# Pairing six tiles of the recurrent branch's gate, and computing two products of nine gate pairs beside the last attention heads

## The chip, the core and the metric

The kernel runs on one core of a Trainium2 chip. The metric is the device time of one execution in microseconds (us). The kernel before takes 2241.29 us, the median of three runs (2237.54 to 2242.33). The execution that the profiler recorded took 2235.38 us; its span, from the first to the last recorded instruction, is 2233.6 us.

Engines: PE (TensorE, matrix products), DVE (VectorE), ACT (ScalarE), POOL (GpSimd), SP (SyncE, which only issues transfers here). Each works through its own list of instructions in a fixed order. DMA transfers are issued from SP, ACT and POOL.

## The reference

One decoder layer on 1024 tokens of width 1024, in float32. A mixer with three branches reads one combined projection of the input; each branch's projection is multiplied by a sigmoid gate, and their sum goes through an output projection, a layer norm, a SwiGLU feed-forward part and a second layer norm. What the change touches, cut from the reference:

```
proj = x @ w_in
lru_x, lru_gate, qb, kb, vb, qc, kc, vc, gates = jnp.split(proj, split_at, axis=-1)
y_a = rglru_branch(lru_x, lru_gate, ...)       # h * gelu(lru_gate), h from an associative scan
y_b = banded_window_attention(...)             # 16 heads, window 128, sinks
y_c = dilated_attention(qc, kc, vc)            # 16 heads, three dilations
branch = jnp.einsum('bsnc,ncd->bsnd', jnp.stack([y_a, y_b, y_c], axis=2), w_branch)
merged = jnp.sum(jax.nn.sigmoid(gates.reshape(bsz, S, 3, D)) * branch, axis=2)
mix = merged @ w_out
```

`lru_gate` is 1024 channels wide, `gates` 3 x 1024.

## The kernel before

**Products in two parts.** Every float32 operand is split into a rounded part `hi` (a CAST on ACT) and the rest `lo` (a subtraction on DVE, in some stages on POOL), and a product is three matmuls: hi x hi, hi x lo, lo x hi. A tile of 128 output channels by 512 tokens with 1024 inputs is 8 x 3 = 24 matmuls of 128x512. A tile of 128 channels over all 1024 tokens is 48.

**Stages, in time.** (1) The recurrent branch's input, convolution, gates and scan. (2) Sliding-window attention. (3) Dilated attention, eight pairs of heads. In 2 and 3 the heads' small matmuls (scores `s`, transposes `pt`, sums `o`) are interleaved with a "fill" of large matmuls `acc`, taken from a stream of weights `W` (class `WeightStream`): `interleave(pipeline(units), fill, ratio)` takes fill worth 1.7 times the heads' estimated matmul time. (4) The gate pairs. (5) The three branch projections with the sum `merged`. (6) The output projection, layer norm, feed-forward part and second layer norm.

**The recurrent branch's gate** (`lg_job`, `lg_evac`, lines 691 to 720) is eight tiles. Tiles 0 and 1 are fill in stage 2; tiles 2 to 7 are the fill of the last pair of dilated heads, 6 x 48 = 288 matmuls. Each half tile is finished on the spot: ACT Square, DVE two operations, ACT Tanh, DVE two operations, store.

**Gate pairs** (class `Pairs`, lines 802 to 965; set up in lines 967 to 1010). Two tiles of `gates` over all tokens would be 96 matmuls. A pair computes them in seven products of 12 matmuls on sums and differences of blocks (Winograd's form of Strassen): a00, s2, s1, s3, a01, s4, a11, that is 84. The weights' sums t1 to t4 are made by POOL (`wsum`, line 864, and line 901), split by ACT and DVE (`wsplit`, lines 874 and 875), all prepared one pair ahead (`prep`, whose steps `run` places at the points `between(i)`). The raw weights of a pair fill the ring `w_raw` (two buffers), so the next pair's weights can be loaded only when the last step of the present pair's preparation has read them. The x operands s1 to s4 are made at the stage's start from x, loaded into `xq` (`load_xq`, `x_sums` lines 770 to 779, `x_split` lines 987 to 992).

A pair can have its products a00 and a01 done ahead (`front_step`, "fronted"): a01 is added onto a00 in the same bank after a copy of a00 was taken, and the pair itself then is five products, 60 matmuls. Before, pairs 0 to 2 of twelve are fronted, at the start of stage 4. Each of a pair's four results goes through a sigmoid on ACT at once (`sig_out`) and to `sg_dram`; stage 5 loads it (`load_sg`, line 1037) and multiplies.

**Order of instructions.** The framework's scheduler sets the order on every engine from the program's order and a simulated timeline, so an instruction can stand far from where the code names it.

**The start of stage 5** (`load_y`, lines 1019 to 1032): the outputs of a branch are loaded from DRAM, eight tiles per half of the tokens, each with its ACT cast and DVE subtraction right behind the load in the code.

## Time and profile before

| | |
|---|---|
| median of three runs | 2241.29 us |
| profiled execution, its span | 2235.38 us, 2233.6 us |
| PE busy | 2173.8 us (97%) |
| DVE, ACT, POOL busy | 1421.0 us (64%), 962.7 us (43%), 539.8 us (24%) |
| chain that ended last, PE's share | 80% |
| stage 4, first matmul of the fronts to the last gate matmul | 943.04 to 1185.3 us |

Busy time counts the union of an engine's instructions. A 128x512 matmul is recorded with about 390 ns, but matmuls overlap, so time per matmul is read from a stretch: its length over its count. "Idle before" is the time that an engine stood still ahead of an instruction, with the instruction that ended the wait.

### The profile page before, as it was taken

What the parts mean: (1) busy time and instruction counts of PE and PEld (TensorE: products, weight loads), DVE (VectorE), ACT (ScalarE), POOL (GpSimd) and SP (SyncE); (2) the same over time, 40 slices, a digit from 0 to 9 for tenths busy, and PEclk for the clock granted to TensorE, in tenths of its full rate; (3) what the DMA queues carried; (4) which work ended last, traced back from release to release, by engine and by line L of the source; (5) the groups of instructions that cost most, each with busy time, mean ns of one, the idle gap of its engine ahead of it and who ended that gap; (6) DMA issues with size and microseconds to landing.
All of it is one profiled execution on the core that took longest, in us unless ns stands there. A gap on an engine that the chain in (4) does not pass through costs nothing.

```text
span 2233.6 us, 29700 instructions
## 1 busy us (share of the span) xinstructions
PE 2173.8 (97%) x11017; PEld 1840.5 (82%) x11017; DVE 1421.0 (64%) x2685; ACT 962.7 (43%) x1825; POOL 539.8 (24%) x493
## 2 busy tenths in 40 slices
PE   8999999999999999989999999999999999999998
PEld 6787888988889888868887888888788888888786
DVE  7888888776777778764444244449665444553735
ACT  4764766665655655543333102223333333342421
POOL 2332222222222133143220000002444433400301
PEclk9999999999999999999999999999999999999999
DMA  5123123112222143343336334244332222254543
GB/s 151 48 81 97 46 67 78 51 48 66 47 58 56 29 107 121 104 147 121 113 123 214 125 113 132 85 147 143 107 104 85 85 85 85 85 193 144 187 160 118
DMA packets 216449, 232.15 MB, mean 104 GB/s; under 512 B 11056, under 2 KB 160624, under 8 KB 216304
## 3 DMA queue, kind: packets, MB, share of 16 engines
q1 hardware_dynamic: 175504, 130.57, 19.2%
q0 software_dynamic: 18336, 57.73, 8.6%
q10 hardware_dynamic: 22464, 41.95, 5.6%
q8 instruction: 87, 1.43, 0.3%
q14 instruction: 58, 0.48, 0.1%
HBM read 170.43 MB, written 49.28 MB: 98 GB/s over the span
## 4 chain that ended last, share of the span: by engine, by line
PE 80%; DVE 8%; issue 4%; DMA 4%; ACT 2%; POOL 1%; SPq 0%; ACTq 0%; DVEq 0%; POOLq 0%
PE acc L186 68%; PE o L186 4%; PE s L186 4%; PE pt L543 4%; DVE xc L386 1%; DVE w_lo L97 1%; POOL t L864 1%; DMA xin<-in_x_t_dram 1%; DMA w_raw<-in_w_branch_dram 1%; DMA yl<-y_dram 1%; DVE r L1217 0%; DVE xc L383 0%; DVE r L1214 0%; DMA w_raw<-in_w_ffn_in_dram 0%; DVE pt_l L548 0%
## 5 line engine op out<-in xcount | busy, mean ns | idle before, releaser
L186 PE MATMUL acc<-xh,w_hi 128*128 128x512 f32 x760 | 303.3, 399 | 12.9 <-ACT w_hi L96 7.8
L186 PE MATMUL acc<-xl,w_hi 128*128 128x512 f32 x760 | 300.5, 395 | 0.0
L186 PE MATMUL acc<-xh,w_lo 128*128 128x512 f32 x760 | 300.0, 395 | 0.0
L96 ACT CAST w_hi<-w_raw 128x1024 fp32r<-128x1024 f32 x127 | 133.5, 1051 | 298.4 <-PE acc L186 256.4
L874 ACT CAST ph<-t 128x512 fp32r<-128x512 f32 x136 | 82.9, 621 | 243.0 <-POOL t L864 149.8
L97 DVE TENSOR_TENSOR w_lo<-w_raw,w_hi 128x1024 fp32r<-128x1024 f32 x89 | 114.4, 1285 | 102.9 <-ACT w_hi L96 102.6
L186 PEld LDWEIGHTS acc<-xh,w_hi 128*128 128x128 f32 x760 | 143.9, 189 | 40.9 <-ACT w_hi L96 7.8
L864 POOL TENSOR_TENSOR t<-w_raw 128x512 f32<-128x512 f32 x68 | 97.0, 1427 | 312.0 <-DMA w_raw<-in_w_ffn_in_dram 194.1
L186 PEld LDWEIGHTS acc<-xh,w_lo 128*128 128x128 f32 x760 | 143.7, 189 | 28.3 <-DVE w_lo L97 0.8
L186 PEld LDWEIGHTS acc<-xl,w_hi 128*128 128x128 f32 x760 | 143.8, 189 | 25.7
L547 ACT CAST pt_h<-pt 128x512 fp32r<-128x512 f32 (+3 forms) x256 | 124.7, 500 | 89.2 <-PE pt L543 84.2
L548 DVE TENSOR_TENSOR pt_l<-pt,pt_h 128x512 fp32r<-128x512 f32 (+3 forms) x256 | 144.3, 572 | 19.5 <-ACT pt_h L547 17.3
L875 DVE TENSOR_TENSOR pl<-t,ph 128x512 fp32r<-128x512 f32 x136 | 102.9, 762 | 82.3 <-ACT ph L874 82.1
L538 POOL DMA_DIRECT2D y_dram<-yp x96 | 52.2, 543 | 418.2 <-DVE yp L537 323.3
L543 PE MATMUL pt<-ident,p 128*128 128x128 f32 x816 | 128.8, 276 | 2.6 <-DVE pt_l L548 1.6
L186 PE MATMUL o<-pt_h,v 128*128 128x256 f32 (+1 forms) x464 | 117.3, 275 | 1.8 <-DVE yp L537 1.8
L630 ACT ACTIVATE p<-p,small 128x128 f32<-128x128 f32 (+7 forms) x128 | 99.5, 778 | 39.8 <-DVE small L627 38.5
L186 PE MATMUL acc<-w_lo,gh 128*128 128x512 f32 x288 | 112.5, 391 | 4.0 <-DVE w_lo L97 3.9
L186 PE MATMUL o<-pt_l,v 128*128 128x256 f32 (+1 forms) x464 | 113.9, 286 | 1.4 <-DVE pt_l L548 1.4
L97 POOL TENSOR_TENSOR w_lo<-w_raw,w_hi 128x1024 fp32r<-128x1024 f32 x38 | 91.4, 2406 | 97.5 <-ACT w_hi L96 91.4
L186 PE MATMUL acc<-w_hi,gl 128*128 128x512 f32 x288 | 112.1, 389 | 0.0
L186 PE MATMUL s<-kh,q 128*128 128x256 f32 (+3 forms) x320 | 103.8, 333 | 1.0 <-DVE small L572 0.5
(378 smaller groups left out, 5825.0 us busy)
## 6 DMA issues: line engine op xcount, KB each, us to landing
w_raw<-in_w_in_dram SPq DMA_DIRECT2D x79, 512.0 KB, 3.9
w_raw<-in_w_ffn_in_dram SPq DMA_DIRECT2D x48, 512.0 KB, 3.8
w_raw<-in_w_ffn_out_dram SPq DMA_DIRECT2D x47, 512.0 KB, 3.7
sg_dram<-e ACTq DMA_DIRECT2D x48, 256.0 KB, 2.7
w_raw<-in_w_branch_dram SPq DMA_DIRECT2D x24, 512.0 KB, 4.7
sg<-sg_dram POOLq DMA_DIRECT2D x24, 512.0 KB, 3.7
g_dram<-e POOLq DMA_DIRECT2D x44, 256.0 KB, 3.2
yl<-y_dram ACTq DMA_DIRECT2D x32, 256.0 KB, 5.7
```

The source lines that it names most:

```text
L96: self.nc.scalar.copy(hi, raw)
L97: self.lo_engine.tensor_sub(lo, raw, hi.bitcast(F32))
L186: pe.matmul(o, a, b, start=start, stop=stop, skip_group_check=True)
L386: dve.scalar_tensor_tensor(xc, xr[:, 1 + j:1 + j + S], vec[:, j * 8 + ct:j * 8 + ct + 1], xc, op0=OP.mult, op1=OP.add)
L538: pool.dma_start(dst, yp[:, :n])
L543: pe.transpose(pt[:, i * P:(i + 1) * P], b, ident)
L547: act.copy(dst_h, v)
L548: dve.tensor_sub(dst_l, v, dst_h.bitcast(F32))
L630: act.activation(p[:, :n], p[:, :n], AF.Exp, bias=m, scale=-1.0, accum_out=sm[:, 1:2])
L864: pool.tensor_tensor(t, a, b, op=op)
L874: act.copy(hi, src)
L875: dve.tensor_sub(lo, src, hi.bitcast(F32))
```

## The change

1. Tiles 2 to 7 of the recurrent branch's gate are no longer fill. They become three pairs (tiles 2 and 3, 4 and 5, 6 and 7) among the gate pairs, at places 3, 6 and 9 of now fifteen, with seven products each. Their four results go through `lg_finish`, a shorter form with three DVE operations and two ACT ones, in tiles `u` and `hh` that lie in `lgt`.
2. The fill of the last dilated heads is now `tail_front` for the gate pairs 3 to 11: products a00 and a01, 24 matmuls each, with the copy of a00 stored to a new DRAM tensor `p1_dram` and the sum to `sg_dram`. All twelve gate pairs are now fronted; the nine get their a00 back by a load one pair ahead.
3. The sigmoid moves out of the gate pairs: raw gates go to `sg_dram`, and stage 5 applies one 128x1024 sigmoid in place after each load (`sigmoids`).
4. `load_y` only issues its loads, not ahead of the latest weight cast of a pair; the casts and subtractions are handed out one at a time (`y_split`). The first is called four pairs before the end, the second half of the first branch inside the first step of stage 5.
5. In `Pairs` the last preparation step is at point 0 instead of 1, the load at 1 instead of 2, the first sums at 3 instead of 4. The difference a01 of the later x tiles goes from POOL to DVE.

```diff
+    def lg_finish(ct, hf, z, u, hh):
+        act.activation(u, z, AF.Square, scale=math.sqrt(0.044715))
+        dve.scalar_tensor_tensor(u, u, 1.0, z, op0=OP.add, op1=OP.mult)
+        act.activation(u, u, AF.Tanh, scale=math.sqrt(2.0 / math.pi))
+        dve.scalar_tensor_tensor(u, u, 1.0, z, op0=OP.add, op1=OP.mult)
+        dve.scalar_tensor_tensor(u, u, 0.5, hh, op0=OP.mult, op1=OP.mult)
+        pool.dma_start(y_dram[0][ct, :, hf * HALF:(hf + 1) * HALF], u)
...
+    def tail_front(g):
+        def f(hi, lo):
+            acc = acc_ps.tile([P, HALF], F32, tag="acc", name="acc")
+            for q, (tag, dst) in enumerate((("kh", p1_dram[g]), ("kl", sg_dram[2 * g, :, :HALF]))):
+                sl = slice(q * HALF, (q + 1) * HALF)
+                yield from quarter(acc, xops[("a00", "a01")[q]], hi[:, sl], lo[:, sl], q == 0)
+                t = att4.tile([P, HALF], F32, tag=tag, name="front")
+                act.copy(t, acc)
+                act.dma_start(dst, t)
+        W.add([gate_cols(g)[0]], [(0, f)])
...
-            for ct in range(KT):
-                if ct not in EARLY:
-                    lg_job(ct)
+            for g in range(NG, NP):
+                tail_front(g)
...
-        pool.tensor_sub(a01, a01, a00)
+        eng.tensor_sub(a01, a01, a00)
...
             def p6():
-                wsplit(j, "b11", b(1, 1))
                 t = raws[j, "t2"]
                 pool.tensor_sub(t, b(1, 0), t)
+                wsplit(j, "b11", b(1, 1))
                 wsplit(j, "t4", t)
...
-                    if i == 1:
+                    if i == 0:
                         cur[6]()
                     elif nxt:
-                        for f in {2: nxt[:1], 4: nxt[1:3], 5: nxt[3:4], 6: nxt[4:6]}.get(i, ()):
+                        for f in {1: nxt[:1], 3: nxt[1:3], 5: nxt[3:4], 6: nxt[4:6]}.get(i, ()):
...
+    kinds = ["g"] * (NP + 3)
+    for i, j in enumerate((3, 6, 9)):
+        kinds[j] = 2 * i + 2
...
+    def pair_out(j, c, hf, src):
+        if j in gid:
+            if hf == 0 and c == 0:
+                t = gate.temp()
+                act.copy(t, src)
+                src = t
+            act.dma_start(sg_dram[2 * gid[j] + c, :, hf * HALF:(hf + 1) * HALF], src)
+        else:
+            u, hh = [t[:, 2 * hf + c, :] for t in lgt]
+            lg_finish(kinds[j] + c, hf, src, u, hh)
...
         for k in range(KT):
-            raw = yl[k].bitcast(F32)
-            act.dma_start(raw, y_dram[n][k, :, hf * HALF:(hf + 1) * HALF])
-            act.copy(yh[k], raw)
-            dve.tensor_sub(yl[k], raw, yh[k].bitcast(F32))
+            d = act.dma_start(yl[k].bitcast(F32), y_dram[n][k, :, hf * HALF:(hf + 1) * HALF])
+            tc.add_manual_dep(d.ins, recent[-1].ins.name, NO_SYNC, reason="not earlier than the pairs' weights")
+            ysplits.append(lambda k=k: split(k))
...
+    def sigmoids():
+        while fresh:
+            t = fresh.pop(0)
+            act.activation(t, t, AF.Sigmoid)
...
+        if i == 3 and j + 1 in gid and gid[j + 1] >= NG:
+            t = gring.tile([P, HALF], F32, tag="p1", bufs=NG, name="p1")
+            act.dma_start(t, p1_dram[gid[j + 1]])
+            gate.front[j + 1] = t
-        if (j, i) == (9, 0):
+        if (j, i) == (len(kinds) - 4, 0):
             load_y(order[0], 0)
+        elif i in (1, 2, 4, 6):
+            y_split()
```

Three places show what the scheduler makes of it.

PE at the end of the dilated heads: `acc` is fill, `s` and `o` are the heads' own. Before, the last fill matmul stands ahead of a 512 wide score of the last head:

```order
L186 MATMUL acc<-xh_94,w_hi 128x512
L186 MATMUL acc<-xl_96,w_hi 128x512
L186 MATMUL acc<-xh_94,w_lo 128x512
L186 MATMUL s<-kh,q 128x512
L186 MATMUL s<-kl,q 128x512
L186 MATMUL o<-pt_h,v 128x256
```

Now, on PE at the same end of the heads, the last fill matmul stands ahead of a 256 wide score:

```order
L187 MATMUL acc<-xh_94,w_hi 128x512
L187 MATMUL acc<-xl_96,w_hi 128x512
L187 MATMUL acc<-xh_94,w_lo 128x512
L187 MATMUL s<-kh,q 128x256
L187 MATMUL s<-kl,q 128x256
L187 MATMUL o<-pt_h,v 128x256
```

The fill ends earlier among the last head's units: in the list before, 41 fill matmuls still follow that 256 wide score, in the new one none.

DVE at the start of stage 4, from the last head's sum `yp` on (`xq` are sums of x, `gs2l` to `gs4l` and `xl` the lo parts of the operands s1 to s4, `pl` of weights). Before:

```order
L778 TENSOR_TENSOR xq<-xq 128x512
L992 TENSOR_TENSOR gs4l<-xq,gs4h 128x512
L776 TENSOR_TENSOR xq<-xq 128x512
L992 TENSOR_TENSOR gs2l<-xq,gs2h 128x512
L992 TENSOR_TENSOR gs3l<-xq,gs3h 128x512
L992 TENSOR_TENSOR gs4l<-xq,gs4h 128x512
L992 TENSOR_TENSOR xl_96<-xq,xh_94 128x512
L777 TENSOR_TENSOR xq<-xq 128x512
L992 TENSOR_TENSOR gs3l<-xq,gs3h 128x512
L992 TENSOR_TENSOR gs2l<-xq,gs2h 128x512
L992 TENSOR_TENSOR gs4l<-xq,gs4h 128x512
L992 TENSOR_TENSOR xl_96<-xq,xh_94 128x512
```

Now, on DVE from the same `xq` on:

```order
L806 TENSOR_TENSOR xq<-xq 128x512
L1029 TENSOR_TENSOR gs4l<-xq,gs4h 128x512
L804 TENSOR_TENSOR xq<-xq 128x512
L1029 TENSOR_TENSOR gs2l<-xq,gs2h 128x512
L1029 TENSOR_TENSOR gs3l<-xq,gs3h 128x512
L1029 TENSOR_TENSOR gs4l<-xq,gs4h 128x512
L807 TENSOR_TENSOR xq<-xq 128x512
L1029 TENSOR_TENSOR xl_97<-xq,xh_95 128x512
L805 TENSOR_TENSOR xq<-xq 128x512
L1029 TENSOR_TENSOR gs3l<-xq,gs3h 128x512
L1029 TENSOR_TENSOR gs2l<-xq,gs2h 128x512
L1029 TENSOR_TENSOR xl_97<-xq,xh_95 128x512
```

Line 807, the difference a01, is new on DVE; the `gs4l` that needs it has moved back, behind the first weights `pl` of a pair.

POOL at the same place, from the last store of the heads on. Before, the two differences of line 779 stand ahead of and among the weights' sums `t`:

```order
L538 DMA y_dram_59<-yp 64x256 x2
L779 TENSOR_TENSOR xq<-xq 128x512
L864 TENSOR_TENSOR t<-w_raw 128x512
L864 TENSOR_TENSOR t<-w_raw,t 128x512
L779 TENSOR_TENSOR xq<-xq 128x512
L901 TENSOR_TENSOR t<-w_raw,t 128x512
```

Now POOL goes from the stores to the weights' sums:

```order
L539 DMA y_dram_59<-yp 64x256 x6
L887 TENSOR_TENSOR t<-w_raw 128x512
L887 TENSOR_TENSOR t<-w_raw,t 128x512
L923 TENSOR_TENSOR t<-w_raw,t 128x512
L887 TENSOR_TENSOR t<-w_raw 128x512 x2
```

The two differences are gone from POOL's list.

## Rows read from the trace of the kernel before

**Rows 1.** Windows: PE, PEld, DVE, ACT, POOL busy (x count), clock, DMA share, GB/s

```profile
915.70:943.04 27.34, 24.05 (x138) 20.71 (x137) 24.03 (x57) 16.76 (x33) 4.14 (x7) 0.94 0.24 78
943.04:985.00 41.96, 32.83 (x134) 25.33 (x134) 29.21 (x41) 22.44 (x41) 17.86 (x9) 0.96 0.50 164
985.00:1185.34 200.34, 200.34 (x876) 165.56 (x877) 88.05 (x122) 72.98 (x117) 55.20 (x42) 0.99 0.38 121
1185.34:1212.00 26.66, 23.27 (x102) 18.65 (x100) 16.48 (x25) 14.65 (x25) 2.17 (x4) 0.98 0.87 302
1212.00:1366.00 154.00, 154.00 (x668) 127.27 (x669) 53.51 (x70) 19.50 (x24) 7.39 (x14) 0.98 0.37 116
```

**Rows 2.** Chain of waits, in order of time: start, length, what (count)

```profile
1049.96 130.12 PE acc L186 x574
```

**Rows 3.** DVE instructions, the last heads: start, length, what

```profile
917.44 0.56 DVE L627 CUSTOM_DVE_ANT_0 p<-s,dil_mask 128x384 f32<-128x384 f32 x1 [0.16 <-PE pt L543]
923.33 0.69 DVE L706 TENSOR_TENSOR gelu__10106<-gelu__10106,z 128x512 f32<-128x512 f32 x1
930.94 1.23 DVE L97 TENSOR_TENSOR w_lo<-w_raw,w_hi 128x1024 fp32r<-128x1024 f32 x1 [0.31 <-ACT w_hi L96]
```

**Rows 4.** PE instructions that waited, start of stage 4

```profile
943.04 0.45 PE L186 MATMUL acc<-xh,w_hi 128*128 128x512 f32 x1
961.79 0.79 PE L186 MATMUL acc<-xh,ph 128*128 128x512 f32 x1 [4.89 <-ACT p L831]
972.00 0.50 PE L186 MATMUL acc<-gs2l,ph 128*128 128x512 f32 x1 [0.73 <-DVE gs2l L992]
985.00 0.50 PE L186 MATMUL acc<-gs2h,ph 128*128 128x512 f32 x1 [3.46 <-ACT ph L874]
```

**Rows 5.** POOL instructions, the last heads and the start of stage 4

```profile
825.39 1.32 POOL L779 TENSOR_TENSOR xq<-xq 128x512 f32<-128x512 f32 x1
953.38 6.40 POOL L779 TENSOR_TENSOR xq<-xq 128x512 f32<-128x512 f32 x1 [8.51 <-DVE xq L778]
981.15 1.80 POOL L864 TENSOR_TENSOR t<-w_raw 128x512 f32<-128x512 f32 x1 [10.96 <-DMA w_raw<-in_w_in_dram]
983.04 1.26 POOL L864 TENSOR_TENSOR t<-w_raw,t 128x512 f32<-128x512 f32 x1
```

**Rows 6.** DVE instructions, start of stage 4

```profile
948.94 0.69 DVE L776 TENSOR_TENSOR xq<-xq 128x512 f32<-128x512 f32 x1 [4.88 <-DMA xq<-in_x_t_dram]
957.37 0.68 DVE L992 TENSOR_TENSOR gs3l<-xq,gs3h 128x512 fp32r<-128x512 f32 x1
957.98 0.68 DVE L992 TENSOR_TENSOR gs2l<-xq,gs2h 128x512 fp32r<-128x512 f32 x1
960.46 1.09 DVE L992 TENSOR_TENSOR gs4l<-xq,gs4h 128x512 fp32r<-128x512 f32 x1 [1.80 <-ACT gs4h L991]
```

**Rows 7.** Chain of waits, a pair's weights: stage 4's second pair, then the feed-forward part

```profile
973.81 7.18 DMA w_raw<-in_w_in_dram
984.33 0.63 ACT ph L874
...
1580.84 1.68 POOL t L901
1585.82 3.62 DMA w_raw<-in_w_ffn_in_dram
1593.70 1.68 POOL t L901
```

**Rows 8.** ACT instructions: start of stage 4, then of stage 5

```profile
954.03 1.28 ACT L978 ACT_TABLE_LOAD   x1
961.64 1.14 ACT L1030 CAST yv<-yv 128x512 fp32r<-128x512 f32 x2
...
1208.18 1.04 ACT L96 CAST w_hi<-w_raw 128x1024 fp32r<-128x1024 f32 x1
```

**Rows 9.** What PE waited for at the start of stage 5: total, times, longest

```profile
PE acc L186 <- ACT w_hi L96: 2.0, 1, 2.0
PE acc L186 <- DVE w_lo L97: 1.4, 1, 1.4
```

More of the change, by code (lines that the diff above doesn't have):

```diff
@@ new lines, in quarter @@
+    def quarter(bank, a, bh, bl, start):
+        ah, al = a
+        for k in range(4):
+            wh, wl = bh[:, k * P:(k + 1) * P], bl[:, k * P:(k + 1) * P]
+            mm(bank, wh, ah[:, k, :], start and k == 0, False)
+            mm(bank, wh, al[:, k, :], False, False)
+            mm(bank, wl, ah[:, k, :], False, k == 3)
+            if k % 2:
+                yield 1296
+    def tail_front(g):
[8 more added lines that the diff above has]
+        W.add([gate_cols(g)[0]], [(0, f)])
@@ L812, in product @@
         def product(self, bank, op, bh, bl, start):
[L814 to L821 removed]
+            return quarter(bank, self.ops[op], bh, bl, start)
         def bank(self):
@@ L1061, in branch_evac @@
             load_sg(i + AHEAD)
+        else:
+            sigmoids()
     def branch_step(i, hf):
@@ L1088, in at @@
     def at(j, i):
-        if (j, i) == (9, 0):
+        if i == 0 and j not in gid:
+            for hf in range(2):
+                for c in range(2):
+                    load_h(kinds[j] + c, hf, lgt[1][:, 2 * hf + c, :])
+        if i == 3 and j + 1 in gid and gid[j + 1] >= NG:
[3 more added lines that the diff above has]
+        if (j, i) == (len(kinds) - 4, 0):
             load_y(order[0], 0)
-        if (j, i) == (11, 4):
+        elif i in (1, 2, 4, 6):
+            y_split()
+        if (j, i) == (len(kinds) - 1, 3):
             W.prefetch(W.n_dma + 2)
-    gate.run(12, at, first, 2)
+    gate.run(len(kinds), at, first, 2)
     gS.close()
@@ L1101, in trunk_kernel @@
         load_sg(i)
-    load_y(order[0], 1)
     for n_, end in enumerate(ends):
-        for _ in W.run(end):
-            pass
+        for i, _ in enumerate(W.run(end)):
+            if (n_, i) == (0, 0):
+                while ysplits:
+                    y_split()
+                load_y(order[0], 1)
+                sigmoids()
+            y_split()
         if n_ % 7 == 1 and n_ < 14:
```

88 lines of the change are left out of this document (41 added, 47 removed).

## The prediction

> **What bounds the kernel now.** I read the page's busy shares first: PE is busy for 97% of the span, and the chain that ended last is 80% PE. So the time is PE's work plus the few places where PE stands still, and an edit on another engine counts only where PE waits for it. The windows by stage then show where that is [rows 1]. From 985.00 to 1185.34, the gate pairs, PE is busy without a gap; from 943.04 to 985.00, the start of stage 4, it is busy for 32.83 of 41.96 us; at the start of stage 5 for 23.27 of 26.66 us. The price of one large matmul comes from the chain: 574 in 130.12 us, 0.2267 us each [rows 2] (the recorded 390 ns overlap). Over the gate pairs it is 200.34 / 876 = 0.2287 us [rows 1]; I use 0.227. Last I read the waits at the start of stage 4, engine by engine [rows 4 to 6].
>
> **The change, part by part.**
>
> *Fill of the last heads.* It goes from 6 x 48 = 288 matmuls to 9 x 24 = 216. The 72 that go are worth 72 x 0.227 = 16.3 us, as long as PE has other work at the heads' end. The order shows that 41 matmuls (9.3 us) are taken from behind the last 256 wide score, where the heads then stand alone. Before, that stretch lasts from 915.70 to 943.04, 27.34 us. Without the 41 it is 27.34 - 9.3 = 18.0 us if the waits in it stay as they are. Two sums bound it from below: PE's own work there is 24.05 - 9.3 = 14.8 us, and DVE's is 24.03 less what is not the heads' (by the kinds of [rows 3]: twelve operations of the recurrent gate, 3 x (0.42 + 0.69 + 0.68 + 0.68) = 7.4; two splits of x, 1.4; a weight's lo part, 1.2), so 14.0 us. Both are below 18.0, so DVE's relief may pay for the missing cover. Against that, scores, transposes and sums of the last units follow each other through three engines; at worst the waits grow by 4 us. I take a loss of 1, with 0 and 4 as ends. The nine copies of a00 on ACT, between a front's two products in one bank, lie beside the heads' matmuls; they are inside these ends.
>
> *Start of stage 4.* Let E be the end of the heads' matmuls, 943.04 before. From there to the second pair's first matmul at 985.00 PE has 72 matmuls of fronts and 60 of the first pair, 132 x 0.227 = 29.9 us, in 41.96 us: 12 us lost, of which 4.89 + 0.73 + 3.46 are the waits of [rows 4] and the rest is the lower clock (0.96 mean) and the ramp. The longest wait, 4.89 us, is for an ACT copy that stands behind a `gs4h` cast, which waits for POOL's difference a01: that took 6.40 us against 1.32 elsewhere [rows 5]. During it DVE ran subtractions on SBUF operands one behind the other, 0.61 us from start to start [rows 6].
> The change puts this difference on DVE, and takes the early casts of y (961.64 in [rows 8]) away from between the weights' casts. What is late next: DVE starts at E + 5.9 as before, when the x tiles land [rows 6]; the order has 17 instructions ahead of the first weight split `pl`, so 17 x 0.61 = 10.4, to E + 16.3. POOL's two sums for it (t1, t2) fall into this train of DVE. If POOL gets no turn beside it, as in the 6.40 us row, they run after it: 1.80 + 1.26 [rows 5], then ACT 0.63 [rows 7] and DVE 0.69, to E + 20.7. PE has finished its fronts at E + 16.3, so it waits 4.4 us, and ends the first pair at E + 34.3. The second pair's weights can be loaded when the first pair's last splits are done, eight DVE instructions later (E + 25.5); the landing took 7.18 us here and 3.62 elsewhere [rows 7], then POOL 3.1, ACT and DVE 1.3: E + 34 to E + 37. I take E + 35 for the second pair's start, against E + 42 before: 7 us gained. Bounds: 11 if POOL runs beside DVE and the load is short; 3 if every transfer takes 7.2 us and a further wait of 2 to 3 us remains.
> Here a rule of the Trainium skill bears ("SBUF — State Buffer", section "Who interferes with whom"): a DVE instruction with two SBUF inputs and a GpSimd instruction that reads SBUF share a port pair, held by one of them for a whole instruction while the other blocks. The 6.40 us row agrees with it. It speaks against taking the whole 11 us: by it POOL's sums pay what the difference paid; without it the gain here would be 11 and the total 19.
>
> *Gate pairs.* Before, from the second pair on: two of five products and nine of seven, 120 + 756 = 876 matmuls. Now eleven of five and three of seven, 660 + 252 = 912. 36 more x 0.227 = 8.2 us of loss. Beside the fill's gain this is the net saving of the algorithm, 36 matmuls. The new pairs' ends (two ACT and three DVE operations per result, four results, about 0.65 us each) come to 8 us of DVE in a pair of 84 x 0.227 = 19.1 us; DVE is busy for 88.05 of 200.34 us here [rows 1], so they lie beside PE. The sigmoids that leave relieve ACT by 48 x 0.6 us, which bounds nothing. What has little room is a pair's weights: in the feed-forward part, where this loop is itself the chain, one turn from `t` to `t` takes 1593.70 - 1580.84 = 12.86 us with a load of 3.62 us in it [rows 7], against 60 x 0.227 = 13.6 us of PE. The new load of a00 and the loads of `hh` come on top of the traffic. I take 1 us of loss; ends 0 and 7.
>
> *Start of stage 5.* PE waits 3.4 us there for the third and fourth weights [rows 9]: their casts stand behind casts of y that wait for loads (1208.18 in [rows 8]; the first branch product ran at 1185.3). Now the x tiles of the first half are free after the last recurrent pair, so eight of those 24 loads and casts come ahead of stage 5. Added in front of the third weight on ACT: a table load, 1.28 us [rows 8], and one or two sigmoids of about 1.1 us, which wait for their own loads. I take a gain of 2; ends: 3.4 gained, 2 lost. Later in stage 5 ACT is busy for 19.50 of 154 us [rows 1], and the 24 sigmoids lie beside PE.
>
> *The rest* (one DVE operation less per half of the two early tiles, the points in `Pairs` for the feed-forward part) falls where PE is busy all the time; 0, within 1 either way.
>
> Sum: -16.3 + 1 - 7 + 8.2 + 1 - 2 = -15.1 us. The profiled execution took 2235.38 us (span 2233.6), so 2220.3 for one like it. The median of the runs is 2241.29, 5.9 above that execution; with it, 2226.
>
> **The rivals.**
>
> *The entry is freed wholly.* POOL runs beside DVE, the heads' end keeps its length, stage 5 starts without a wait: -16.3 - 11 + 8.2 - 3.4 = -22.5, 2219. For it: POOL's other sums next to busy DVE took 1.3 to 1.8 us. Against it: the 6.40 us.
>
> *The covers fail.* The last heads alone lose 4, the entry gives 3, stage 5's start loses 2 behind the sigmoids: -16.3 + 4 - 3 + 8.2 + 1 + 2 = -4.1, 2237, no change that can be told. For it: in the naked end of the heads each unit needs three engines in turn; the first sigmoid waits for a transfer at a time when the transfers moved 302 GB/s [rows 1]. Against it: DVE has 10 us less to do there.
>
> *The weights' loop becomes the bound* (the other side). Eight pairs that follow a five-product pair are new to this loop (places 5, 6, 8, 9 and 11 to 14). If their loads take the 7.18 us of [rows 7] instead of 3.62, a turn is 16.4 us, 2.8 above PE's 13.6: 8 x 2.8 = 22.4 lost, +7.3 in all, 2249. It decides from a turn of 13.6 + 15.1 / 8 = 15.5 us on. For it: the new transfers, and POOL's stores of `u` that stand ahead of the sums and wait for DVE. Against it: the pairs that run so before show no gap in PE [rows 1], and 7.18 was measured beside the y loads that move away.
>
> **Chances.** The forecast 0.55 (its own range 2220 to 2232), the freed entry 0.17, failing covers 0.18, the weights' loop 0.10, a part of it with small losses. A measurement of this kernel can tell about 0.2%, 4.5 us, from no change. Faster by more: 0.55 + 0.17 + about half of the failing covers, 0.81; within: 0.12; slower: 0.07. The range for 8 in 10 reaches from the freed entry with some run-to-run spread, 2214, into the loop's case, 2243.
>
> **What would show it.** In the changed profile: 36 large matmuls fewer in all; the stretch from the last 256 wide score to the heads' end near 18 us; from there to the second pair's first matmul near 35 us, with POOL's first `t` long or late beside DVE; PE without gaps in the gate pairs and the turns of `t` at 13.6 us; at the start of stage 5 under 1.5 us of waiting. The forecast is wrong if PE waits for `ph` or `pl` in every five-product pair, or if the heads' end takes over 22 us.

## The result and the profile after

The changed kernel takes 2242.52 us (median of 20 runs, 2237.01 to 2248.11) against 2236.32 us for the kernel before in the same series: ratio 1.0022, 95% interval [1.0012, 1.0031]. It is slower by about 5 us. The forecast was 15.1 us less than before, 2226 from a median of 2241.29 that rested on three runs. The profiled execution took 2241.2 us with a span of 2239.4 us, 5.8 above the span before, so the two profiles can stand for the two medians.

The windows by stage of the changed kernel, in the columns of [rows 1]: the last heads alone, the start of stage 4 up to the second pair, the pairs from there on, the start of stage 5, its later part.

```profile
912.00:929.36 17.36, 12.39 (x80) 9.66 (x81) 13.97 (x39) 9.47 (x21) 2.09 (x4) 1.00 0.18 54
929.36:965.81 36.45, 32.74 (x135) 25.58 (x134) 23.00 (x35) 16.06 (x30) 13.84 (x8) 0.95 0.51 161
965.81:1193.08 227.27, 214.63 (x913) 174.87 (x912) 130.00 (x192) 67.18 (x113) 80.01 (x66) 0.97 0.49 155
1193.08:1219.74 26.66, 25.54 (x112) 20.50 (x111) 16.16 (x26) 15.54 (x24) 2.16 (x4) 1.00 0.84 294
1219.74:1368.74 149.00, 149.00 (x659) 123.39 (x658) 51.90 (x68) 35.08 (x38) 7.41 (x14) 1.00 0.38 117
```

The second and third line answer the question. The heads end 13.68 us earlier (929.36 against 943.04), and the second pair starts 36.45 us after that, not 41.96. Then the pairs, which ran without a gap before, take 227.27 us instead of 200.34, with 12.6 us in which PE stands still and a clock of 0.97. (PE's list puts 15 branch matmuls ahead of the last gate product; 1193.08 is the end of the gate pairs less these 15 x 0.2267 us.)

| stretch, profiled executions | forecast | measured |
|---|---|---|
| up to the heads' end | -16.3 + 1 = -15.3 | -13.7 |
| heads' end to the second pair | -7 | -5.5 |
| second pair to the last gate product | +8.2 + 1 = +9.2 | +26.9 |
| stage 5 (to the output projection: 268.98, now 262.98) | -2 | -6.0 |
| the rest (779.28, now 783.34) | 0 | +4.1 |
| sum | -15.1 | +5.8 |

PE's waits in the pairs, in the form of [rows 4]; in brackets the idle time and what ended it. `ph` and `pl` are the hi and lo parts of a pair's weights or of their sums `t`, `b11` is the last block of the raw weights, and `e` stands for the sums that DVE makes of a pair's products.

```profile
949.90 0.50 PE L187 MATMUL acc<-gs2h,ph 128*128 128x512 f32 x1 [3.19 <-ACT ph L897]
978.10 0.50 PE L187 MATMUL acc<-gs2h,ph 128*128 128x512 f32 x1 [1.25 <-ACT ph L897]
1026.87 0.80 PE L187 MATMUL acc<-gs2h,ph 128*128 128x512 f32 x1 [4.71 <-ACT ph L897]
1079.15 0.50 PE L187 MATMUL acc<-gs2h,ph 128*128 128x512 f32 x1 [2.98 <-ACT ph L897]
1130.40 0.50 PE L187 MATMUL acc<-gs2h,ph 128*128 128x512 f32 x1 [3.02 <-ACT ph L897]
1176.58 0.50 PE L187 MATMUL acc<-gs2h,ph 128*128 128x512 f32 x1 [0.67 <-ACT ph L897]
```

Each is the first product (s2) of a pair whose weights are not there. Two of them (949.90 and 978.10) belong to the start of stage 4 and its third pair. The three long ones behind those come two places after each recurrent pair (places 5, 8 and 11). Behind each, the granted clock is down for some time, here behind the first:

```profile
1020.00:1030.00 10.00, 5.29 (x17) 3.97 (x16) 6.70 (x10) 1.77 (x3) 5.31 (x6) 0.79 0.55 194
1030.00:1040.00 10.00, 10.00 (x40) 8.12 (x39) 5.05 (x8) 2.81 (x4) 0.81 (x1) 0.86 0.46 135
1060.00:1070.00 10.00, 10.00 (x46) 8.29 (x45) 7.75 (x12) 4.22 (x8) 3.14 (x3) 1.00 0.28 80
```

In the second line PE is busy throughout and does 40 matmuls, in the third 46: these are means of 10 us, between the levels of 1.2 and 2.4 GHz. From 1026.87 to 1030.00, right behind the wait, the granted clock is 0.50; behind the other two it is 0.71 from 1079.15 to 1085.00 and 0.64 from 1130.40 to 1135.00. So 26.9 us are 36 matmuls (8.2), 12.6 of waits, and the remaining 6.1 are matmuls that took longer than 0.2267 us each, 7.9 us in all against 1.8 before.

What makes ph late is a loop. Here the chain of waits of the changed kernel (start, length, what), a turn near the end of the pairs where nothing disturbs it:

```profile
1155.54 0.61 DVE pl L898
...
1156.21 3.67 DMA w_raw<-in_w_in_dram
...
1160.05 1.30 POOL t L887
...
1161.42 1.30 POOL t L887
...
1164.16 1.68 POOL t L923
1165.84 1.26 POOL t L887
...
1168.39 0.70 DVE pl L898
...
1169.14 3.90 DMA w_raw<-in_w_in_dram
...
1173.21 1.30 POOL t L887
```

The last split of a raw tile (`pl` at 1168.39) frees it, the next pair's weights are loaded into it, POOL makes the sums, and the splits follow: 13.16 us from `t` to `t`. A pair of five products is 13.6 us of PE. The loop is the chain here, though PE waits for it only 0.67 us, at 1176.58. Now POOL's first `t` of the pairs around the first recurrent pair, and then around the second:

```profile
961.67 1.29 POOL L887 TENSOR_TENSOR t<-w_raw 128x512 f32<-128x512 f32 x1 [7.05 <-DMA w_raw<-in_w_in_dram]
974.75 1.29 POOL L887 TENSOR_TENSOR t<-w_raw 128x512 f32<-128x512 f32 x1 [5.75 <-DMA w_raw<-in_w_in_dram]
...
1003.59 1.29 POOL L887 TENSOR_TENSOR t<-w_raw 128x512 f32<-128x512 f32 x1 [8.33 <-DMA w_raw<-in_w_in_dram]
...
1023.57 1.26 POOL L887 TENSOR_TENSOR t<-w_raw 128x512 f32<-128x512 f32 x1 [4.67 <-DMA w_raw<-in_w_in_dram]
...
1040.74 1.29 POOL L887 TENSOR_TENSOR t<-w_raw 128x512 f32<-128x512 f32 x1 [9.94 <-DMA w_raw<-in_w_in_dram]
1055.89 1.29 POOL L887 TENSOR_TENSOR t<-w_raw 128x512 f32<-128x512 f32 x1 [8.11 <-DMA w_raw<-in_w_in_dram]
1075.85 1.26 POOL L887 TENSOR_TENSOR t<-w_raw 128x512 f32<-128x512 f32 x1 [4.63 <-DVE u L697]
1092.58 1.29 POOL L887 TENSOR_TENSOR t<-w_raw 128x512 f32<-128x512 f32 x1 [9.49 <-DMA w_raw<-in_w_in_dram]
```

Undisturbed 13.1 us, across a recurrent pair 20.0 (1003.59 to 1023.57, 1055.89 to 1075.85). One recurrent pair with its two gate pairs is 84 + 60 + 60 matmuls, 46.2 us of PE; the three turns from 1040.74 to 1092.58 take 51.8. The long turn itself, on ACT and then on DVE and SP:

```profile
1010.93 0.62 ACT L897 CAST ph<-t 128x512 fp32r<-128x512 f32 x1 [3.52 <-POOL t L887]
1011.46 0.63 ACT L694 ACTIVATE u<-e 128x512 f32<-128x512 f32 x1
...
1014.90 0.63 ACT L696 ACTIVATE u<-u 128x512 f32<-128x512 f32 x1 [0.87 <-DVE u L695]
1015.44 0.60 ACT L897 CAST ph<-w_raw 128x512 fp32r<-128x512 f32 x1
```

```profile
1016.77 0.69 DVE L898 TENSOR_TENSOR pl<-w_raw,ph 128x512 fp32r<-128x512 f32 x1
```

```profile
1017.52 0.37 SPq L882 DMA_DIRECT2D w_raw<-in_w_in_dram  x1
```

The cast of b11, which has had its data since 1003.6, stands in ACT's list behind Square and Tanh of the recurrent pair's finish; DVE's half of it comes 13.2 us after the first `t` (8.6 us in an undisturbed turn), and the load takes another 6.1 us from its issue to the next `t` (3.7 undisturbed).

### The profile page after: what moved, and what is told of

The parts are those of the page before. It is cut to its first block, busy times and chain, and to the rows that moved or that the text cites. A ratio compares the mean times of both kernels' runs of the same rounds, so it can differ in the third digit from the quotient of the medians.

```text
span 2239.4 us, 29667 instructions
## 1 busy us (share of the span) xinstructions
PE 2170.8 (97%) x10981; PEld 1834.5 (82%) x10981; DVE 1424.7 (64%) x2695; ACT 969.7 (43%) x1826; POOL 559.5 (25%) x506
## 3 DMA queue, kind: packets, MB, share of 16 engines
q1 hardware_dynamic: 184864, 135.28, 19.9%
## 5 line engine op out<-in xcount | busy, mean ns | idle before, releaser
L187 PE MATMUL acc<-xh,w_hi 128*128 128x512 f32 x688 | 274.6, 399 | 13.0 <-ACT w_hi L96 6.9
L187 PE MATMUL acc<-xl,w_hi 128*128 128x512 f32 x688 | 272.1, 395 | 0.0
L187 PE MATMUL acc<-xh,w_lo 128*128 128x512 f32 x688 | 271.6, 395 | 0.0
L897 ACT CAST ph<-t 128x512 fp32r<-128x512 f32 x148 | 89.7, 620 | 309.6 <-POOL t L887 219.7
L887 POOL TENSOR_TENSOR t<-w_raw 128x512 f32<-128x512 f32 x74 | 109.0, 1472 | 313.8 <-DMA w_raw<-in_w_ffn_in_dram 193.8
L898 DVE TENSOR_TENSOR pl<-t,ph 128x512 fp32r<-128x512 f32 x148 | 111.3, 759 | 113.0 <-ACT ph L897 112.9
L187 PEld LDWEIGHTS acc<-xh,w_hi 128*128 128x128 f32 x688 | 130.4, 189 | 38.8 <-ACT w_hi L96 6.9
L187 PEld LDWEIGHTS acc<-xh,w_lo 128*128 128x128 f32 x688 | 130.1, 189 | 25.5 <-DVE w_lo L97 0.8
L187 PEld LDWEIGHTS acc<-xl,w_hi 128*128 128x128 f32 x688 | 130.4, 190 | 23.5
L97 POOL TENSOR_TENSOR w_lo<-w_raw,w_hi 128x1024 fp32r<-128x1024 f32 x41 | 98.9, 2412 | 113.0 <-ACT w_hi L96 106.9
```

The costliest lines, as they stand in the source:

```text
L97: self.lo_engine.tensor_sub(lo, raw, hi.bitcast(F32))
L187: pe.matmul(o, a, b, start=start, stop=stop, skip_group_check=True)
L887: pool.tensor_tensor(t, a, b, op=op)
L897: recent[:] = [act.copy(hi, src)]
L898: dve.tensor_sub(lo, src, hi.bitcast(F32))
```

## The experiments

Seventeen kernels were run. In the table "pairs" is the time from the heads' end to the last gate product, as above, and "waits" PE's idle time in it, both from one profiled execution; ratios are against the kernel before, which ran beside each group. The executions of one kernel spread over 4 to 14 us, so a difference of a few us in the last two columns decides nothing by itself; that of early is the slowest of its ten, that of spread_pe the fastest of its ten. The "first part" of the change means its items 1 and 2 together, the recurrent pairs and the fronts beside the last heads.

| run | median us | ratio [95%] | pairs us | waits us |
|---|---|---|---|---|
| before | 2236.3 to 2238.3 | | 242.3 | 9.1 |
| changed | 2242.5 | 1.0022 [1.0012, 1.0031] | 263.7 | 16.3 |
| pe_order | 2249.1 | 1.0054 [1.0034, 1.0073] | 264.8 | 19.7 |
| late | 2244.2 | 1.0025 [1.0010, 1.0039] | 262.3 | 17.2 |
| no_finish | 2244.2 | 1.0034 [1.0023, 1.0046] | 259.8 | 15.1 |
| spread_pe | 2241.7 | 1.0025 [1.0010, 1.0041] | 258.0 | 12.2 |
| early | 2238.8 | 1.0002 [0.9988, 1.0017] | 255.9 | 12.3 |
| best1 | 2241.9 | 1.0018 [1.0005, 1.0032] | 260.9 | 17.7 |
| half | 2229.2 | 0.9948 [0.9928, 0.9968] | 237.6 | 5.5 |
| one_h | 2239.9 | 1.0009 [0.9999, 1.0019] | 260.9 | 14.7 |
| lg345 | 2244.5 | 1.0042 [1.0029, 1.0054] | 261.8 | 15.1 |
| lg345e | 2236.5 | 1.0007 [0.9995, 1.0019] | 257.7 | 11.7 |
| k2 | 2235.9 | 0.9992 [0.9976, 1.0008] | 258.7 | 15.2 |
| half_a01 | 2230.9 | 0.9967 [0.9954, 0.9980] | 236.1 | 4.9 |
| raw4 | 2232.2 | 0.9989 [0.9977, 1.0001] | 250.1 | 8.0 |
| raw4_all | 2242.6 | 1.0029 [1.0016, 1.0042] | 265.7 | 18.5 |
| k2r | 2228.8 | 0.9968 [0.9954, 0.9983] | 247.7 | 8.6 |
| half_s | 2231.5 | 0.9971 [0.9961, 0.9982] | 238.5 | 6.8 |
| k2s | 2226.0 | 0.9953 [0.9936, 0.9970] | 247.3 | 9.3 |

### First theories: the lists

PE's list, too, looks guilty: behind each recurrent pair it holds the next pair's s2 and s1 ahead of the present pair's s4 and a11. Theories: O (PE's order), R (the late return of the raw tile), D (transfers).

**pe_order.**

```diff
     def mm(o, a, b, start, stop):
-        pe.matmul(...)
+        m = pe.matmul(...)
+        if floor:  # set for s2 and s1 of a pair to the last matmul of the pair before
+            tc.add_manual_dep(m.ins, floor[0].ins.name, NO_SYNC, reason="pair after pair")
```

> Changed kernel, with one addition: the first two products of a pair (s2, s1) are tied behind the last product (a11) of the pair before it on TensorE; nothing else is tied. Theory O (TensorE's own list is the cause: behind each recurrent pair it holds the next pair's s2 and s1 ahead of this pair's s4 and a11, whose weights are ready): the waits of 4.71, 2.98 and 3.02 us go, each to under 0.5 us, and with them the slow clock behind them (6.0 us more in this stage than in the kernel before): about 2242.5 - 10.7 - 6 = 2226 us. Theory R (the raw weights are given back late, since their last split stands behind the recurrent pair's finish on ScalarE and VectorE, so the next load is late whatever TensorE does meanwhile): a wait of 2 to 5 us stays in each of the three places, only at another product; 2238 to 2243 us.

Measured 2249.12 us, the slowest of all. The wait moved to s4:

```profile
1031.88 0.76 PE L189 MATMUL acc<-gs4h,ph 128*128 128x512 f32 x1 [6.18 <-DVE e L959]
```

s4 adds onto the bank of s1, and DVE's sum that has to read this bank first stands in DVE's list behind the next pair's first split, which waits for the same load:

```profile
1030.44 0.69 DVE L904 TENSOR_TENSOR pl<-t,ph 128x512 fp32r<-128x512 f32 x1 [3.35 <-ACT ph L903]
```

O falls as far as PE's list alone is meant; DVE's list holds a like order. The wait stayed and moved to another product, as R said for this run, though at 6.18, 0.96 and 2.99 us, and the time came out 6 us above R's.

**late.**

```diff
-            lg_finish(kinds[j] + c, hf, src, u, hh)
+            later.append(lambda: lg_finish(..., gate.split))  # run at point 0 of the next pair,
+            # Square and the first product tied behind that pair's last split on ACT and DVE
```

> Changed kernel, with the finish of a recurrent pair (Square, Tanh and three products for each of four tiles) handed out behind the next pair's last two weight splits, and tied there on ScalarE and VectorE; TensorE's list keeps the next pair's s2 and s1 ahead of this pair's s4 and a11 in all three places. Theory R (late return of the raw weights): the split that gives them back comes at about 1012.8 instead of 1017.5, the next load lands 4.6 us earlier, and the three waits shrink to under 0.7 us each: about 2226 us. Theory O (TensorE's order alone): the waits stay at 2.5 us or more each, 2238 to 2243 us. A third, D (the loads of h and the stores of y that run at that time slow the weights' load, 5.9 us instead of 3.6): the load stays slow and at least 2 us of each wait remain, 2232 to 2238 us.

2244.17 us. The three waits at those places did go, and the turn behind the recurrent pair fell to 13.8 us, as R said; but the next turn rose to 19.8, and PE now waits for the sums `e` (8.5 us in all) and for ph elsewhere. The delay was handed on, not removed.

**no_finish** (leaves the Gelu of six tiles out).

```diff
-            lg_finish(kinds[j] + c, hf, src, u, hh)
+            lg_short(...)     # u = 0.5 * z * hh, and the store
```

> Changed kernel without the Gelu of the six tiles of the recurrent pairs: their finish is one product on VectorE (z times h) and the store; Square, Tanh and the two other products are left out. The loads of h and the stores of y stay, and TensorE's list still holds part of the next pair's s2 ahead of s4. If the instructions of the finish are the cause (R, or VectorE being full in the pair behind a recurrent one): the three waits fall under 1 us each, about 2226 us. If the transfers are the cause (D): they stay at 2 us or more, 2235 to 2242 us.

2244.21 us, waits of 3.66 and 2.62 us still at the first two places. There the finish's instructions are not needed for the stall. At the third place, behind which neither kernel loads an h, the wait for ph is gone (1.98 us for `e` at 1139.62 remain) and the turn is 14.8 us instead of 18.8; POOL's `t` there, in the changed kernel and here:

```profile
1107.62 1.28 POOL L887 TENSOR_TENSOR t<-w_raw 128x512 f32<-128x512 f32 x1 [7.99 <-DMA w_raw<-in_w_in_dram]
1126.38 1.65 POOL L887 TENSOR_TENSOR t<-w_raw 128x512 f32<-128x512 f32 x1 [3.44 <-DVE e L946]
```

```profile
1105.10 1.29 POOL L891 TENSOR_TENSOR t<-w_raw 128x512 f32<-128x512 f32 x1 [8.40 <-DMA w_raw<-in_w_in_dram]
1119.92 1.29 POOL L891 TENSOR_TENSOR t<-w_raw 128x512 f32<-128x512 f32 x1 [2.88 <-DMA w_raw<-in_w_in_dram]
```

The turn at the first place, on POOL and on SP:

```profile
1021.12 1.26 POOL L891 TENSOR_TENSOR t<-w_raw 128x512 f32<-128x512 f32 x1 [5.91 <-DMA w_raw<-in_w_in_dram]
```

```profile
1013.84 0.37 SPq L886 DMA_DIRECT2D w_raw<-in_w_in_dram  x1
```

The raw tile comes back 2.8 us sooner in its turn than in the changed kernel (11.2 us after the first `t` instead of 13.9), but 7.3 us pass from the load's issue to the next `t`, beside the loads of h and the stores of y: a turn of 18.5 us instead of 20.0.

**spread_pe.** The finish in two halves (Square, (u+1)z and 0.5 z h in the pair; Tanh and the last product handed out over the next two pairs), with the order of pe_order.

```diff
+            lg_first(src, u, hh)
+            later.append(lambda: lg_second(kinds[j] + c, hf, u, hh))
```

> A version meant as a mend: the finish of a tile is cut in two, first what reads z (Square, (u+1)z, and 0.5 z h into h's place), in the pair itself, and later Tanh and the last product, one tile at each of two points of the next two pairs; and TensorE keeps pair behind pair as in the run that ties its products. R and O both say that the three waits go: 2242.5 - 10.7 - 6 = about 2226 us, the sum that was forecast. If VectorE is simply too full in these pairs, waits of 1 to 3 us stay, 2232 to 2240 us.

2241.68 us. The three waits for ph did go, with 0.66 us for `e` in each of these places and 1.95 and 2.44 us behind the third, and yet the median is that of the changed kernel. Turns across a recurrent pair are still 18.1 to 18.3 us. The scheduler drew most of the second halves forward again.

### The loop itself

**early.** The loop made shorter.

```diff
+                if soon:       # fronted pairs: right after t1 (written over b00) and t2
+                    wsum(j, "t3", b(1, 1), b(0, 1), OP.subtract)
+                    wsplit(j, "b11", b(1, 1))
```

> Changed kernel, with a shorter weights' loop for the pairs of five products: the fourth sum (t3) and the split of b11 come right after the first two sums, and the first sum is written over b00, so that it takes no buffer; the last reader of the second raw tile is then done about 7.3 us after the first sum instead of 9.3 us, and 13 us where a recurrent pair's finish stood ahead. Theory L (the turn of the weights' loop, 13.1 to 13.5 us undisturbed against 13.6 us of TensorE, has no margin, so that each delay of it behind a recurrent pair is paid in full: three turns take 51.8 us where TensorE needs 46.2 us): the turns fall to 12 us or less where undisturbed and to under 16 us behind a recurrent pair, the waits for ph fall from 10.7 to under 3 us, about 2228 us. Theory O (lists on TensorE and VectorE): waits of 2 to 4 us stay per recurrent pair, 2238 to 2245 us.

2238.83 us: the ratio falls from 1.0022 to 1.0002 (the two intervals just overlap), in the direction of theory L and about a quarter of its size. Waits of 1.2 to 2.0 us remain at two of the places, and the first pairs lose: 3.54 and 2.95 us at their starts.

**best1.** early + late + pe_order, and the loads of h tied behind the recurrent pair's own splits.

```diff
+                    tc.add_manual_dep(d.ins, recent[-1].ins.name, NO_SYNC, reason="behind the splits")
```

> All mends at once: the shorter weights' loop of the run above, the finish behind the next pair's splits, TensorE pair after pair, and the loads of h tied behind the recurrent pair's own splits on ScalarE's queue (before, they stood behind the last finish and held the queue until VectorE was through with the old h). Theory L: the loop is under TensorE's time everywhere, waits in the pairs under 5 us with those of the start, about 2225 us. If what counts is VectorE's work in the pair behind a recurrent one (its finish, splits and sums: some 13 us of 13.6): waits for sums (e) of 1 to 3 us stay in three places, 2230 to 2238 us.

2241.86 us, no better than early alone (the intervals overlap). Behind the first pair PE's waits are now for DVE's sums (1.3 + 0.7 us in each of three places), as the second case named, with a time 4 us above it.

**half.** The change without its first part.

```diff
-            for g in range(NG, NP):
-                tail_front(g)
+            for ct in range(KT):
+                if ct not in EARLY:
+                    lg_job(ct)
...
+    kinds = ["g"] * NP         # no recurrent pairs; fronted: j < NG
```

> The changed kernel without its first part: the six recurrent tiles are made beside the last heads again and nine gate pairs have seven products, as in the kernel before; the rest of the change stays (x sums on VectorE, order of the loads at the entry, points of preparation, sigmoids in the branch stage, loads and splits of y handed out). In the comparison of the two profiles these other parts took 5.5 us off the start of the gate pairs and 6.0 us off the branch stage. If they do the same here: 2237 - 11 = about 2226 us, faster than both. If the gain in the branch stage hangs on the pairs that waited (TensorE's waits gave ScalarE the time for the splits of y): 2230 to 2234 us.

2229.21 us, ratio 0.9948. Everything else in the change is worth about 9 us by the medians and 12 by the ratio; the first part alone costs 13 by the medians (2242.5 less 2229.2) and 17 by the ratios.

**one_h** (leaves out h for two of three recurrent pairs).

```diff
-        if i == 0 and j not in gid:
+        if i == 0 and j == 3:
```

> Changed kernel, where h is loaded for the first recurrent pair alone and the other two multiply by the old h (left out: eight loads of 256 KB). Theory D (those loads slow the weights' load, and their place on ScalarE's queue holds up the splits behind it): the weights' load behind the first two recurrent pairs takes about 4 instead of 5.9 us and the waits there shrink by 2 us or more each, about 2235 us. Theory L with the late split as its cause: under 1 us each, 2239 to 2243 us.

2239.89 us, inside theory L's range, with waits between the two cases: turns of 17.9 and 18.1 instead of 20.0, waits of 3.01 and 1.96 instead of 4.71 and 2.98. The loads of h are a part of the delay there, about 2 us a turn. They are not needed for it: behind the third recurrent pair neither kernel loads an h, and the turn is 18.8 us in the changed kernel and 20.1 here, with waits of 3.02 and 3.73 us. With no_finish, either the finish or the loads of h alone make a turn of about 18 us or more; these are single executions.

**lg345** and **lg345e.**

```diff
-    for i, j in enumerate((3, 6, 9)):
+    for i, j in enumerate((3, 4, 5)):
```

> Changed kernel with one number changed: the three recurrent pairs stand at places 3, 4 and 5 instead of 3, 6 and 9, so that two of them are followed by another pair of seven products (19.0 us of TensorE) and only one by a pair of five (13.6 us). Theory L (a turn of the weights' loop behind a recurrent pair, about 20 us, is paid where TensorE's pair is 13.6 us): behind places 3 and 4 the wait shrinks to 1 us or none, behind place 5 it stays at 3 to 5 us: 10.7 us of waits become 4 to 6, about 2234 us. If the finish itself (VectorE, or the order of the lists) costs TensorE the time whatever pair follows: no change, 2240 to 2244 us. Against it here: there is one set of buffers for h, so the next h can only be loaded once the last finish is through, which may hold up ScalarE's queue.

> The same places 3, 4 and 5, with the shorter weights' loop (t3 and the split of b11 early), two sets of buffers for h, and its loads tied behind the splits. Theory L: no wait for ph behind recurrent pairs over 2 us, pairs about 6 us shorter than in the run with the places alone, about 2228 us.

2244.47 and 2236.45 us. In lg345 the waits behind places 3 and 4 shrank to 1.51 and 1.14 us (now for `e`) and stayed 3.11 behind place 5, as theory L said, yet one of 2.82 us appeared among plain pairs of five products (1127.13), and nothing was gained. That nine five-product pairs in a row leave the loop no pair in which to catch up is the likely reason; it was not tried. With the shorter loop 8 us came back, short of the 2228 expected.

**k2.** Two recurrent pairs instead of three, three gate pairs with seven products, one behind each recurrent pair: `spec = "fffLufLufuffff"` (f fronted, u seven products, L recurrent).

> Two thirds of the change's first part, laid out by theory L: two recurrent pairs (four tiles) among the gate pairs, two tiles left beside the heads, six gate pairs with fronts beside the heads, three with seven products; behind each recurrent pair stands a gate pair of seven products. Against the run without the first part: beside the heads 96 + ... matmuls fewer: 288 - (96 + 144) = 48 fewer (-10.9 us), in the pairs 24 more (+5.4 us), so -5.4 us. Theory L: the turns of about 20 us fall on pairs of 19.0 us, waits under 2 us each, about 2229 - 5 + 2 = 2226 us. If the recurrent pairs cost as much wherever they stand: 2229 + 4 = 2233 us or more.

2235.91 us. Waits shrink behind the recurrent pairs (1.19 and 2.80 us, for sums) but 5.8 us for ph come in the last places. Theory L's number was 10 us too low.

**half_a01.** half, with the difference a01 back on POOL.

> The run without the change's first part, with the last of the x sums at the entry (a01 of the third and fourth quarter) back on GpSimd, as in the kernel before, where it took 6.40 us beside VectorE's work instead of 1.32 us. The prediction put 3 to 11 us on the start of the gate pairs, most of it on this: then this run is 3 us or more slower than the one with a01 on VectorE, at its second pair. If the earlier loads or the order of ScalarE's list did it: within 1 us.

2230.93 us, against 2229.21 an overlap of the intervals. PE's waits in the pairs of half_a01 and of half (what was waited for, total, times, longest):

```profile
PE acc L187 <- ACT p L870: 4.8, 1, 4.8
```

```profile
PE acc L187 <- ACT ph L913: 4.6, 2, 3.2
PE acc L187 <- DVE e L967: 0.9, 2, 0.7
```

With a01 on POOL there is one wait, of the kind of the 4.89 us of [rows 4]; on DVE there are others of about the same sum. From the heads' end to the second pair's first matmul half_a01 takes 37.5 us and half 36.1, against 41.96 before. So the place of a01 is worth 1 or 2 us at most, not clear of the scatter, and most of the gain comes without it. What half_a01 has gained over [rows 4] is that the wait of 3.46 us at the second pair is gone; the earlier points of preparation are the likely cause, but they were not tried alone.

**raw4.** Two more raw tiles, in a buffer that stands empty until y is loaded; pairs at odd places up to 9 load there.

```diff
+                if self.spare and j % 2 and j < 11:
+                    t = self.spare[0][:, 2 * i:2 * i + 2, :].rearrange("p a b -> p (a b)")
+    gate.spare.append(vpool.tile([P, 4, HALF], F32, tag="v", name="w_raw2"))
```

> Changed kernel with two more raw weight tiles (a buffer that stands empty from the x sums until y is loaded): the pairs at odd places up to 9 load into these, so that a load can start a whole pair earlier. Nothing else is changed. Theory L (the weights' loop bounds the pairs): the load falls out of the loop, the three waits behind the recurrent pairs shrink to under 1 us each, and the wait of 1.25 us in the third pair goes: about 2242.5 - 11 - 6 = 2226 us. Theory V (ScalarE's and VectorE's lists: the splits themselves come too late, whatever the load does): the waits for ph stay at 2 to 5 us each, 2238 to 2243 us.

2232.16 us, ratio 0.9989: 10 us less than the changed kernel from this edit alone, though 6 above theory L's figure. From the second pair on PE waits for weights by more than 0.3 us only here:

```profile
965.05 0.50 PE L187 MATMUL acc<-gs2h,ph 128*128 128x512 f32 x1 [0.74 <-ACT ph L901]
1136.81 0.51 PE L187 MATMUL acc<-gs2h,ph 128*128 128x512 f32 x1 [2.34 <-ACT ph L901]
1164.80 0.50 PE L187 MATMUL acc<-gs2h,ph 128*128 128x512 f32 x1 [0.45 <-ACT ph L901]
```

The waits behind the first two recurrent pairs are gone; of those left, the first stands at the start and the other two where the extra tiles end. POOL's first sum of such a pair no longer waits for a load:

```profile
1012.87 1.68 POOL L891 TENSOR_TENSOR t<-w_raw 128x512 f32<-128x512 f32 x1 [4.04 <-DVE pl L902]
```

The finish and the transfers are all still there; what was taken away is that the load must wait for the last split. This shows the loop, and in it the load that must wait, as the cause of the waits.

**raw4_all.** raw4 with late, pe_order and the tied loads of h.

> The two more raw tiles, with the finish behind the next pair's splits, the loads of h tied behind the recurrent pair's own splits, and TensorE pair after pair. Theory L and V together: no wait over 1 us in the pairs behind the start, about 2224 us. If VectorE is simply full behind a recurrent pair: waits for its sums (e) of 1 to 3 us in three places, 2230 to 2236 us.

2242.59 us: the ties give all of it back, in waits for DVE's sums (14.3 us in all). Where the loop is free, these orders are pure loss; the second case of the expectation holds for the waits, with a time 6 us above it.

**k2r, k2s and half_s.** k2 with the raw4 edit; k2 and half with the two raw tiles already for the first pair (even places).

> The two-thirds version (two recurrent pairs, each followed by a gate pair of seven products) with the two more raw tiles. Theory L: 2229 - 10.9 + 5.4 = 2224 us, waits behind the recurrent pairs under 1 us. If waits of the loop are not what it lost before (2235.9 us): unchanged at 2234 to 2238 us.

> The run without the first part (2229.2 us), with a third and fourth raw tile: the first gate pair's weights are loaded into a buffer that the x sums leave empty, four half products earlier, and the pairs at even places up to 6 load there too. If the wait of 3.24 us for ph at the first pair, and of 1.37 us behind it, are the raw tiles' (the load waits for the fronts' weights to leave): both go, with the slow clock behind them, 2229 - 4.6 - 2 = about 2223 us. If it is the x sums or the splits on ScalarE and VectorE: a wait of 3 us or more stays there, 2228 to 2230 us.

> The two-thirds version with the same two raw tiles from the first pair on (even places up to 8). If the raw tiles bound both the start and the pairs behind the recurrent ones: 2228.8 - 5.7 (waits at the start in the run with raw tiles from the second pair on) - 2 = about 2222 us. If the start stays as it is and only the pairs gain: 2228 to 2230 us, as that run.

2228.80, 2231.46 and 2225.97 us. Theory L's figure for k2r was 2224. Freeing the loop gains k2 7 us. The start did not move: half_s has one wait of 6.78 us where half had 3.24 and 1.37. The load was not freed earlier (issued at 955.93, in half at 952.76), since its buffer holds x until DVE has split it, and DVE's train of x sums only starts when x lands, after the heads' end; the second of the two loads then took 7.3 us to land, in half the one at 952.76 took 3.8:

```profile
950.99 0.69 DVE L820 TENSOR_TENSOR xq<-xq 128x512 f32<-128x512 f32 x1 [6.42 <-DMA xq<-in_x_t_dram]
...
963.63 0.70 DVE L823 TENSOR_TENSOR xq<-xq 128x512 f32<-128x512 f32 x1
```

k2s beats both kernels: ratio 0.9953 [0.9936, 0.9970]. The simpler half, at 0.9948, cannot be told from it.

## Why the prediction was wrong

**The step that failed** is "Gate pairs ... I take 1 us of loss; ends 0 and 7". It measured 18.7 (26.9 less the 8.2 of 36 matmuls): 12.6 of waits, and 6.1 of slower matmuls behind them, for which the sum had no term. The text had the loop and its size, a turn of 12.86 us against 13.6, and priced it as a margin of 0.7 us. Besides that, two things were left out. First, it compared one undisturbed turn with one pair; the new program disturbs each third turn by 7 us, and with pairs at 13.6 and turns at 13.1 to 13.5 nothing wins that back before the next one. Second, it had the finish of the recurrent pairs as "8 us of DVE in a pair of 19.1 us ... they lie beside PE". Most of it lay in the following pair, of 13.6 us (first Square at 1011.46, last product ended at 1023.6; the recurrent pair's matmuls end at 1013.8), on the two engines that also return the raw tile: DVE's average load (130.00 of 227.27 us) says nothing of that.

**The rival that came true** is "the weights' loop becomes the bound", given 0.10. It said +7.3 us and the span rose by 5.8; its 22.4 us of loss compare with 18.7. It decided from turns of 15.5 us on, and the turns of a group of three averaged 17.3. Two of its reasons fell: no load took 7.18 us in the changed kernel (3.5 to 5.9 from issue to landing), and eight pairs did not lose 2.8 us each, but three places lost 3 to 4.7 us and the clock behind them. The evidence against it, "no gap in PE" in [rows 1], came from nine seven-product pairs of 19 us, which had 6 us in hand, and from only two of five products, with no recurrent pair to disturb them.

**The heads' end**: -13.7 for -15.3. The stretch from the last 256 wide score took 19.9 us where 18.0 was forecast, and the loss of cover was about 2.6 us instead of 1, inside its ends of 0 and 4. The step was right.

**The start of stage 4**: -5.5 for -7, E + 36.45 for E + 35, inside 3 to 11, and POOL's first sum came as written. It was to be long or late beside DVE's train:

```profile
941.74 6.12 POOL L887 TENSOR_TENSOR t<-w_raw 128x512 f32<-128x512 f32 x1 [10.54 <-DMA w_raw<-in_w_in_dram]
```

6.12 us for an instruction of 1.3, until DVE's train ended. In half_a01 the difference a01 took 7.00 us in the same place. The Trainium skill's rule ("SBUF — State Buffer", section "Who interferes with whom") that the two engines share a port pair which one locks agrees with these rows in who waits for whom, but not in how long: it holds the pair for one instruction, and here POOL's sum ended only after eight more instructions of DVE, 0.60 us apart. What the prediction credited the gain to was wrong: with the difference a01 back on POOL most of the gain is still there (half_a01), so it came from elsewhere, likely from the earlier points of preparation, which were not tried alone. That the number came close is in part luck.

**Stage 5**: -6.0 for -2, outside its ends. The two waits of 3.4 us became 1.1, as forecast; a third of 0.9 us at 1372.59 and the slower clock behind them (2.8 us), which the sum had left out, went with them. But this stretch varies: in the seventeen other profiles of this stage it took 261.1 to 269.1 us, 264.4 in the mean, so -4.5 is the better figure.

**The rest**: +4.1 for 0. The only code that differs here is the preparation in `Pairs` (its points, and the order within its last step), which the feed-forward part uses too. Up to the last matmul, output projection and feed-forward took 770.1 to 779.7 us in the seventeen other profiles, 770.5 before and 774.7 after: the difference lies inside the scatter of single executions, though these seventeen all have the new points and the kernel before stands near their lower end. Its cause stays open.

**What stays open.** Even with the loop freed (raw4), the full first part is no better than none (2232.2 against 2229.2): the heads end 12.7 us earlier than in half, and the pairs are 12.5 longer, of which 8.2 are matmuls and the rest waits and clock. Whether those can be saved too stays open. Items 3 to 5 of the change were only run together (half), so their 9 us are not divided among them. The shares of the 7 us by which a turn grows are not settled either: the late split is 4.6 us of it by the rows, the slower load 2.4, yet taking away one (late, no_finish, one_h) mostly left a long turn at the same or the next place.

## What to carry to other kernels

A ring of buffers that is refilled by its own last reader is a loop; compare its turn, with every disturbance that the new program puts on the engines in it, with the shortest piece of work that runs beside it, and sum over the group of turns that repeats, not one turn. Work that shortens a stage on the bounding engine (seven products to five) lowers the bar for everything beside it. When such a loop stalls, a further buffer that takes the load out of it (10 us here) did more than any order of the lists.

## What was not expected of the hardware

A load of 512 KB for the pairs took 3.5 us from issue to landing at best in the changed kernel (issued at 971.05, with 151 GB/s moved in all meanwhile) and 5.9 at worst (1017.52, 248 GB/s), and in no_finish 7.1 us (1013.84, 251 GB/s). The four waits of 2.98 to 4.71 us of PE in the pairs were each followed by matmuls at a lower granted clock, which cost more than half of what the waits cost, on top of them: 10.7 us beside 16.3 after, 4.7 beside 9.1 before (the length of the pairs, less the waits, less 0.2267 us for each of 1044 and 1008 matmuls).
